# Merge stage on two pairs of PSUM banks, gated outputs transposed one gate later, output projection by halves of its inputs

## The chip, the cores and the metric

The kernel runs on one core of a Trainium2 chip. The metric is device time in microseconds (us). TensorE (PE) multiplies matrices and transposes; VectorE (DVE), ScalarE (ACT) and GpSimd (POOL) work elementwise; SyncE (SP) issues the transfers from HBM, in its program's order. Each engine works through its own instruction list in order and waits at semaphores for the others.

## The reference, cut to what matters

Two layers over 256 tokens of width 1024, all in float32. Each layer runs three causal mixers on one input projection, merges them by sigmoid gates, projects, normalises, and then runs a mixture of 32 experts.

```
proj = h @ w_in[l]           # all mixers' inputs, dn_gate, hg_gate, gate_logits
y_a = mla_branch(...)              @ w_br_a[l]
y_b = (rms_norm(dn_o) * silu(dn_gate)) @ w_br_b[l]   # gated DeltaNet
y_c = (rms_norm(hg_o) * silu(hg_gate)) @ w_br_c[l]   # HGRN2
g_a, g_b, g_c = split(sigmoid(gate_logits))
mixed = (g_a*y_a + g_b*y_b + g_c*y_c) @ w_out[l]
h = layer_norm(ALPHA*h + mixed)
# router: top-1 of 4 groups, then top-2 of its 8 experts; SwiGLU experts
h = layer_norm(ALPHA*h + hier_moe(h))
```

## The kernel before, in words

The 256 tokens are two tiles of 128 rows (t = 0, 1). A float32 product is made from three products of rounded halves (`mm3`, L261 to L263: high*high, low*high, high*low). A weight is split into its halves on the way: `split` lets ACT make the high half `wh` (L249) and DVE subtract to get the low half `wl` (L250); for the four names in `POOLED` POOL does the subtraction. `wh` and `wl` have two buffers each, so a split can run one piece ahead of PE. A tile of weights is 1 MB; in the merge stage it is split in two pieces, and each piece feeds 12 products (two token tiles, two blocks of 128 inputs, three products), which are called a chunk here.

The order per layer: the mixers (`seq` in `layer`); then branch a's gate and product in two column halves (`merge_branch`, c = 0, 1); the output gates of the two other branches, dn_gate and hg_gate (`gates`, `rows512`); `branch_gate` for dn and hg, which multiplies the normalised branch output by its gate (L1119), transposes it on PE in 16 blocks (L1126) and casts and splits the result (ACT L1128, DVE L1129); `router_sums` (a DVE reduction L568, a small product L571); `merge_branch` for b and c; the output projection `project_out` with the weights wo0 and wo1 (one for each half of the output columns); the router; the experts (`moe`, nine groups of experts, "quads"). glb0 names the gate of branch b, column half 0; br_b0 the product of branch b for that half. A merge step is: gate products, ACT tanh into `sg`, branch products, DVE (1 + sg) * product (L1277), POOL add to `mix` (L1279). `mix_turned` transposes `mix` into the projection's input, half by half of its columns.

PSUM results for t = 0 and t = 1 go to the banks named "pa" and "po", one bank each (`ps`, tag "pa"); the next step that uses them waits until ACT or DVE has read the last. Three banks are named "pm" and three "pb"; transposes and small products alternate between these names.

Weights come through SP's list in a fixed order into buffers: four in the pool `wp`, thirteen more that open when the mixers' memory closes (`open_prefetch`, `NPRE`), and five more that open at the end of the merge stage. A tile of one of the pools is loaded again when its last reader has finished; SP stands in line for that reader. The weight row tile `rows` (ln1_g and ln1_b for the first layer norm's scale, used by POOL's `scaled`, L376 and L377) uses such a buffer too. The order of instructions on each engine comes from a list scheduler with its own estimates; `issue_after` holds an instruction behind another.

Of the kernel before, what the change touches and what calls it, by code (L numbers as in the profile page):

```python
# [10 lines left out]
F32 = mybir.dt.float32  # L11
# [4 lines left out]
OP = mybir.AluOpType  # L16
# [91 lines left out]
class Trunk:  # L108
    def __init__(self, ctx, tc, A, out, dbg=None):
        self.ctx, self.tc, self.nc, self.A, self.out, self.dbg = ctx, tc, tc.nc, A, out, dbg or {}  # L110
        nc = self.nc
        pool = lambda n, b=1, **k: ctx.enter_context(tc.tile_pool(name=n, bufs=b, **k))
        self.cp = pool("consts")
        self.hp = pool("hidden")
        self.wp = pool("weights")
        self.wtiles, self.bufs = {}, {self.wp: self.NBUF}
        self.pk = pool("banks", space=PSUM)
        self.ctx_p, self.pp, self.nps, self.npa = ctx.enter_context(ExitStack()), None, 0, 0

    def cst(self, n, rows=slice(0, 128)):  # L120
        o, w = HOFF[n]
# [18 lines left out]
        return pool.tile([128, 512], F32, name="ps_" + tag, tag=tag, bufs=self.banks[tag])  # L140


    POOLED = {"cq.0", "cq.1", "gla00.0", "dn_gate1.1"}
    NBUF, NPRE = 4, 13
    BANKS, MIX_BANKS, MOE_BANKS = {"pa": 1, "pm": 3}, {"po": 1, "pb": 3}, {"sum": 4}
    NB = {"a2": 4, "a4": 7, "d2": 8, "d4": 7, "d8": 1, "wh": 2, "wl": 2, "o4": 4, "sg": 4}
# [140 lines left out]

    def wide(self, l, n, act):

        ps = [self.ps("pa") for _ in range(TB)]  # L290
        for i in range(2):
            self.wide_half(ps, l, n, act, i)
        return ps

    def wide_half(self, ps, l, n, act, i, ahead=False):
        self.dense_tm(ps, self.w(l, f"{n}{i}").rearrange("p (k c) -> p k c", k=4), act, f"{n}{i}", 4 * i, KT, ahead)
# [292 lines left out]
    def layer(self, l):  # L589
        tc, side = self.tc, dict(side="right")  # L590
        with ExitStack() as cl, ExitStack() as cr:
            self.ctx_l = cl
            self.sp = cr.enter_context(tc.tile_pool(name=f"split{l}", bufs=1, **side))
            self.gp = cr.enter_context(tc.tile_pool(name=f"merge{l}", bufs=1, **side))
            xp = cr.enter_context(ExitStack())
            hp = xp.enter_context(tc.tile_pool(name=f"x{l}", bufs=1, **side))
            oc = cr.enter_context(ExitStack())
            self.op = oc.enter_context(tc.tile_pool(name=f"o{l}", bufs=1, **side))
            with tc.tile_pool(name=f"mix{l}", bufs=1) as mp:
                self.mp = mp  # L600
                self.open_small(mp, 256)
                if l == 0:
                    rope, src = self.buf("d8", [128, 8, T]), self.A["positions"]
                    self.nc.sync.dma_start(rope[:, 0].bitcast(I32),
                                           bass.AP(tensor=src.tensor, offset=src.offset, ap=[[0, 128], [1, T]]))
                    self.issue(self.wp)
                self.mixer_consts(l, mp)
                if l == 0:
                    for _ in range(self.NBUF - 2):
                        self.issue(self.wp)  # L610
                    self.vrows = self.small_weights(l)
                self.mla_weights(l)
                gb = [x.rearrange("p h t -> p (h t)") for x in self.o4(F32)]
                for x, n in zip(gb, "gb"):
                    self.bcast_row(x, self.A["ln_in_" + n] if l == 0 else self.A["ln2_" + n][l - 1], D)
                self.hT = [hp.tile([128, KT, T], F32R, name=n, tag=n) for n in ("hTh", "hTl")]
                diag = self.gp.tile([128, 4, 128], F32, name="sg", tag="sg", bufs=self.NB["sg"])
                for t in range(TB):
                    self.nc.vector.tensor_scalar(diag[:, t], self.ident, self.hrs[:, t], None, op0=OP.mult)
                self.transposed(self.h, self.hT, self.gb0, tmp=lambda: self.buf("d2", [128, 2, T]), scale=diag)  # L620
                if l == 0:
                    with tc.issue_after(self.latest(self.nc.tensor)):
                        self.warm(8)
                    with tc.issue_after(self.last_lo.ins):
                        self.rope_tables(rope)
                self.router_weights(l)
                self.mix = self.gp.tile([128, TB, D], F32, name="mix")

                self.pq = self.ps("pm")
                self.chunk_cm(self.pq, l, "cq")  # L630
                seq = "dn_decay mla h0 dn_keys dn_inverse dn_queries h1 " \
                      "dn_values hg_forget hg_project hg_local dn_scan hg_scan"
                for n in seq.split():
                    f, a = (self.mla_heads, (int(n[1]),)) if n in ("h0", "h1") else (getattr(self, n), ())
                    self.bank = "pb" if n[:2] == "dn" else "pm"
                    f(l, mp, *a)
                    if f == self.mla:
                        with tc.issue_after(self.last_exp.ins):
                            for t in range(TB):
                                self.nc.scalar.activation(self.h[:, t], self.h[:, t], AF.Copy, scale=self.hrs[:, t])  # L640
                self.bank = None

                with tc.issue_after(self.latest(self.nc.gpsimd)):
                    self.scaled(self.h, gb[:1], gb[1:], self.nc.gpsimd)
                    if l == 0:
                        self.nc.gpsimd.tensor_copy(self.bits[:, 1], self.cst("ustrict"))
                self.dump(f"h2_{l - 1}", self.h.rearrange("p t d -> p (t d)"))
                self.merge_branch(l, "a")
                self.gates(l, mp)
                self.branch_gate(l, mp, "dn", self.dn_o)  # L650
                self.branch_gate(l, mp, "hg", self.hg_o)
                self.router_sums(self.last_gate.ins)
            self.pw = self.open_prefetch(f"prefetch{l}", self.NPRE)
            self.merge_branch(l, "b")
            def between():

                self.mixS = [hp.tile([128, 8, T], F32R, name=n, tag=n) for n in ("hTh", "hTl")]
                self.mix_turned(0)

            self.merge_branch(l, "c", between)  # L660

            oc.close()
            self.open_prefetch(f"more{l}a", 2)

            def free():
                xp.close()
                self.open_prefetch(f"more{l}b", 2)

            self.project_out(l, free)
            cr.close()  # L670
            self.open_prefetch(f"more{l}c", 1)
            with tc.tile_pool(name=f"h1_{l}", bufs=1, **side) as xp, tc.tile_pool(name=f"moe{l}", bufs=1, **side) as ep, \
                    ExitStack() as yc:
                self.moe(l, xp, ep, yc, self.h)
# [430 lines left out]
    def branch_gate(self, l, mp, n, o):  # L1105
# [10 lines left out]
            nc.vector.tensor_scalar(ss, ss, 1.0 / 128, 4 * EPS, op0=OP.mult, op1=OP.add)  # L1116
        self.rsqrt(rs, ss, self.small([128, 8]))
        for i in range(8):
            self.last_gate = nc.vector.scalar_tensor_tensor(ov[:, i], ov[:, i], rs[:, i:i + 1], gv[:, i], op0=OP.mult,  # L1119
                                                            op1=OP.mult)  # L1120
        oT = self.o4()
        for i in range(0, 4, 2):
            ps = self.ps()
# [133 lines left out]
            self.dump_oT(l, "mla")  # L1257


    def merge_branch(self, l, br, between=None):  # L1260


        nc = self.nc
        oT = self.oT[{"a": "mla", "b": "dn", "c": "hg"}[br]]
        for c in range(2):
            sg = [self.gp.tile([128, 512], F32, name="sg", tag="sg", bufs=self.NB["sg"]) for _ in range(TB)]
            for s, ps in zip(sg, self.wide(l, f"gl{br}{c}", self.hT)):
                nc.scalar.activation(s, ps, AF.Tanh, scale=0.5)
            if c and between:
                between()  # L1270
            n = f"br_{br}{c}"
            ps = [self.ps("pa") for _ in range(TB)]
            self.dense_tm(ps, self.w(l, n).rearrange("p (k c) -> p k c", k=4), oT, n, 0, 4)
            self.done(l, n)
            for t in range(TB):
# [15 lines left out]
    def project_out(self, l, free):  # L1291
        nc, A = self.nc, self.A

        r, st = self.h, self.stats(2)

        pr = self.ps()

        def route(t, c):
# [6 lines left out]
                nc.tensor.matmul(pr[:, 64 * t:64 * t + 36], x[:, k], self.rw[:, 4 * c + k, 0:36],  # L1305
                                 start=(t + c + k == 0), stop=(c + k == 4), skip_group_check=True)

        for c in range(2):
            ps = [self.ps("pa") for _ in range(TB)]
            for i in range(2):  # L1310
                self.wide_half(ps, l, f"wo{c}", self.mixS, i, c + i == 2)
                if c == 0 and i == 0:
                    self.mix_turned(1)
                if c == 1 and i == 0:
                    for t in range(TB):
                        route(t, 0)
            if c:
                free()
            cs = slice(512 * c, 512 * c + 512)
            for t in range(TB):  # L1320
                nc.vector.scalar_tensor_tensor(r[:, t, cs], self.h[:, t, cs], 2 * ALPHA, ps[t], op0=OP.mult, op1=OP.add)
                nc.vector.bn_stats(st[:, t, c], r[:, t, cs])
        for t in range(TB):
            route(t, 1)
        self.logits, self.st1 = pr, st


    def router(self, l, ep, x, xc):
# [446 lines left out]
```

## Time and profile before

| | before |
|---|---|
| median of 3 runs | 1159.97 us (1159.62 to 1160.34) |
| profiled execution, its own time | 1160.61 us |
| its span | 1158.8 us |
| PE busy | 1059.3 us, 91% |
| DVE, ACT, POOL busy | 50%, 37%, 14% |
| HBM over the span | 262 GB/s |

The two layers are alike: the second runs some 570 us after the first through the same steps. In layer 0 the gates' products end at 255.2 us, merge b and c run to 329 us, the output projection to 357.4 us, the router to 371 us and the experts to about 570 us. The start of a product minus the start of the one before it is the time that a product takes; what is above the usual value is a stall, also where the wait that the profile shows is shorter.

### The profile page before, as it was taken

How to read it: one execution, taken by the hardware profiler on the slowest of the kernel's cores; microseconds unless marked ns; L12 is line 12 of the kernel's file. 1: busy time of each engine (PE TensorE's matmuls, PEld its weight loads, DVE VectorE, ACT ScalarE, POOL GpSimd, SP SyncE). 2: the span in 40 equal slices, each digit the busy share in tenths (PEclk: the TensorE clock that was granted, in tenths of full speed). 3: DMA queues.
4: the chain of work that ended last, by engine and by line, in shares of the span. 5: the costliest groups of instructions: out<-in, count | busy, mean ns of one | idle time of the engine just before them, and what ended most of it. 6: DMA issues, size and time to landing. Idle time of an engine off the chain costs nothing. (4 is left out here: it accounts for less than half of the span.)

```text
span 1158.8 us, 21407 instructions
## 1 busy us (share of the span) xinstructions
PE 1059.3 (91%) x8896; PEld 775.6 (67%) x8896; DVE 576.9 (50%) x1269; ACT 427.3 (37%) x788; POOL 162.7 (14%) x146
## 2 busy tenths in 40 slices
PE   7999999999999998777889999999999999977775
PEld 5888987777777664434378889777777766543442
DVE  7677754575556422111276876645754562321114
ACT  5764632554445211111067545235444351211111
POOL 2111025101210400000020110450021112000001
PEclk9999999999999999898899999999999999989997
DMA  7632250549965999999983214315599679999994
GB/s 231 200 107 73 91 165 2 169 158 359 424 271 220 410 425 426 426 426 427 366 230 106 74 46 138 110 38 182 196 411 374 251 270 425 426 425 426 427 426 190
DMA packets 104706, 305.58 MB, mean 264 GB/s; under 512 B 20962, under 2 KB 48028, under 8 KB 79516
## 3 DMA queue, kind: packets, MB, share of 16 engines
q1 hardware_dynamic: 104604, 304.15, 68.4%
q8 instruction: 72, 1.18, 0.4%
q14 instruction: 30, 0.25, 0.1%
HBM read 303.08 MB, written 1.05 MB: 262 GB/s over the span
## 5 line engine op out<-in xcount | busy, mean ns | idle before, releaser
L250 DVE TENSOR_TENSOR wl<-w,wh 128x1024 fp32r<-128x1024 f32 x150 | 187.0, 1248 | 161.5 <-ACT wh L249 161.0
L249 ACT CAST wh<-w 128x1024 fp32r<-128x1024 f32 x158 | 165.7, 1049 | 217.7 <-PE ps_po L263 74.7
L1602 PE MATMUL ps_pa<-w,xg 128*32 128x256 f32 x2304 | 175.1, 436 | 59.0 <-DMA w<-in_exp_w_up_dram 29.4
L1602 PEld LDWEIGHTS ps_pa<-w,xg 128*32 128x32 f32 x2304 | 88.0, 125 | 140.4 <-DMA w<-in_exp_w_up_dram 38.2
L1614 DVE SCALAR_TENSOR_TENSOR hm<-ps_pa,ws,hm 128x256 f32<-128x256 f32 x18 | 8.7, 484 | 203.5 <-ACT hm L1613 203.3
L1613 ACT ACTIVATE hm<-ps_pa 128x256 f32<-128x256 f32 x18 | 6.9, 384 | 221.8 <-PE ps_pa L1602 221.8
L261 PE MATMUL ps_pa<-wh,hTh 128*128 128x512 f32 x176 | 71.2, 405 | 2.0 <-ACT hTh L254 0.7
L261 PE MATMUL ps_po<-wh,hTh 128*128 128x512 f32 x176 | 71.2, 405 | 1.9 <-ACT hTh L254 0.7
L262 PE MATMUL ps_po<-wl,hTh 128*128 128x512 f32 x176 | 70.5, 401 | 2.1 <-DVE wl L250 1.6
L262 PE MATMUL ps_pa<-wl,hTh 128*128 128x512 f32 x176 | 70.5, 401 | 2.1 <-DVE wl L250 1.6
L1635 PE MATMUL ps_pm<-w,hmT 128*32 128x512 f32 x576 | 70.8, 595 | 1.3 <-issue 1.3
L263 PE MATMUL ps_pa<-wh,hTl 128*128 128x512 f32 x176 | 70.0, 398 | 0.2 <-DVE hTl L255 0.2
L263 PE MATMUL ps_po<-wh,hTl 128*128 128x512 f32 x176 | 69.9, 397 | 0.2 <-DVE hTl L255 0.2
L1552 PEld LDWEIGHTS ps_pm<-P,h1c 128*128 128x128 f32 x576 | 66.8, 192 | 2.2 <-ACT res L1350 1.0
L1552 PE MATMUL ps_pm<-P,h1c 128*128 128x128 f32 x576 | 67.3, 275 | 0.0
L1561 ACT ACTIVATE xg<-ps_pm,gb 128x128 f32<-128x128 f32 x72 | 32.9, 458 | 71.7 <-DVE xg L1559 71.7
L1574 POOL TENSOR_TENSOR Pw<-P,small 128x128 f32<-128x128 f32 x32 | 12.4, 405 | 306.9 <-PE ps_pm L1581 227.9
L1279 POOL TENSOR_TENSOR mix<-mix,sg 128x512 f32<-128x512 f32 x16 | 28.3, 1792 | 155.4 <-DVE sg L1277 155.4
L1559 DVE TENSOR_SCALAR xg<-ps_pm,gb 128x128 f32<-128x128 f32 x72 | 29.4, 408 | 41.2 <-PE ps_pm L1552 32.2
L263 PE MATMUL ps_po<-hTh,wl 128*128 128x256 f32 (+1 forms) x168 | 48.7, 290 | 0.9 <-DVE wl L250 0.5
L263 PE MATMUL ps_pa<-hTh,wl 128*128 128x256 f32 (+1 forms) x168 | 48.9, 291 | 0.5 <-DVE wl L250 0.5
L261 PE MATMUL ps_pa<-hTh,wh 128*128 128x256 f32 (+1 forms) x168 | 49.2, 293 | 0.0
(442 smaller groups left out, 2134.9 us busy)
## 6 DMA issues: line engine op xcount, KB each, us to landing
w<-in_exp_w_gate_dram SPq DMA_DIRECT2D x66, 1024.0 KB
w<-in_exp_w_up_dram SPq DMA_DIRECT2D x66, 1024.0 KB
w<-in_exp_w_down_dram SPq DMA_DIRECT2D x64, 1024.0 KB
w<-in_w_in_dram SPq DMA_DIRECT2D x58, 1024.0 KB
w<-in_w_out_dram SPq DMA_DIRECT2D x8, 1024.0 KB
w<-in_w_br_a_dram SPq DMA_DIRECT2D x4, 1024.0 KB
w<-in_w_br_b_dram SPq DMA_DIRECT2D x4, 1024.0 KB
w<-in_w_br_c_dram SPq DMA_DIRECT2D x4, 1024.0 KB
```

What stands on the lines that cost most here:

```text
L249: nc.scalar.copy(v(hi), raw)
L250: engine.tensor_tensor(v(lo), raw, v(hi).bitcast(F32), op=OP.subtract)
L261: mm(ps, a[0], b[0], start=start, stop=False, skip_group_check=True)
L262: mm(ps, a[0], b[1], start=False, stop=False, skip_group_check=True)
L263: mm(ps, a[1], b[0], start=False, stop=stop, skip_group_check=True)
L1279: nc.gpsimd.tensor_tensor(mv, mv, sg[t], op=OP.add)
L1552: nc.tensor.matmul(ps[:, 128 * k:128 * k + 128], xc[:, t, 4 * h + k], Ps[q][:, t], start=(t == 0), stop=(t == 1))
L1559: nc.vector.tensor_scalar(xg[:, k], o, g, b, op0=OP.mult, op1=OP.add)
L1561: nc.scalar.activation(xg[:, k], o, AF.Identity, scale=g, bias=b)
L1574: self.pool_last = nc.gpsimd.tensor_tensor(e(Pw[:, t]), e(P[:, t]), w, op=OP.mult)
L1602: nc.tensor.matmul(pg[32 * e:32 * e + 32, FF * n:FF * n + FF], xgs[q][k // 4][:, k % 4, 32 * e:32 * e + 32], w[:, FF * k:FF * k + FF], sta ...
L1635: nc.tensor.matmul(ps[c][32 * e:32 * e + 32], hmT[:, i, 32 * e:32 * e + 32], ws[e][:, D * i + 512 * c:D * i + 512 * c + 512], start=(i == ...
```

## The change

What it does: `pair` gives a step either the banks pa and po or two of the pb banks, in turn, once merge a is done; so a gate and the branch product behind it lie on different banks. `branch_gate` ends at the multiplication; the transposes and casts (`branch_turned`) come behind the products of gate glb0, on pm banks. `project_out` takes half 0 of the inputs for both wo0 and wo1, then half 1 for each. The router's sums stand behind `hg_project`, in the scans. The subtraction for gla00's first and dn_gate1's second piece goes from POOL to DVE. The thirteen prefetch buffers open after the first gate of branch b.

```
-    POOLED = {"cq.0", "cq.1", "gla00.0", "dn_gate1.1"}
+    POOLED = {"cq.0", "cq.1"}
...
     def wide(self, l, n, act):
-        ps = [self.ps("pa") for _ in range(TB)]
+        ps = self.pair()
...
+    def pair(self):
+        self.npair += 1
+        return [self.ps("pb" if self.scans_done and self.npair % 2 else "pa") for _ in range(TB)]
...
                     f(l, mp, *a)
+                    if n == "hg_project":
+                        self.router_sums(self.latest(self.nc.vector))
...
                 self.merge_branch(l, "a")
+                self.scans_done = True
                 self.gates(l, mp)
                 self.branch_gate(l, mp, "dn", self.dn_o)
                 self.branch_gate(l, mp, "hg", self.hg_o)
-                self.router_sums(self.last_gate.ins)
+                first = self.merge_gate(l, "b", 0)
+                self.bank = "pm"
+                self.branch_turned(l, "dn", self.dn_o)
+                self.branch_turned(l, "hg", self.hg_o)
+                self.bank = None
             self.pw = self.open_prefetch(f"prefetch{l}", self.NPRE)
-            self.merge_branch(l, "b")
+            self.merge_branch(l, "b", gate=first)
...
-        for c in range(2):
-            ps = [self.ps("pa") for _ in range(TB)]
-            for i in range(2):
-                self.wide_half(ps, l, f"wo{c}", self.mixS, i, c + i == 2)
-                if c == 0 and i == 0:
-                    self.mix_turned(1)
-                if c == 1 and i == 0:
-                    for t in range(TB):
-                        route(t, 0)
-            if c:
-                free()
+        def residual(c):
             cs = slice(512 * c, 512 * c + 512)
             for t in range(TB):
...
+        ps = [self.pair() for _ in range(2)]
+        for c in range(2):
+            self.wide_half(ps[c], l, f"wo{c}", self.mixS, 0)
+            if c == 0:
+                self.mix_turned(1)
+        self.wide_half(ps[0], l, "wo0", self.mixS, 1)
+        residual(0)
+        for t in range(TB):
+            route(t, 0)
+        self.wide_half(ps[1], l, "wo1", self.mixS, 1, True)
+        free()
+        residual(1)
```

DVE, layer 0, between the splits of glb0's first and second chunk, before. The last row is the subtraction for the second chunk; `a_2193` is the hg branch's output, `o_2667` the low half of the dn branch's transposed output.

```order
L317 SCALAR_TENSOR_TENSOR a_2555<-a_2555,ps_po 128x512 [waits Activation_49]
L1129 SCALAR_TENSOR_TENSOR o_2667<-ps_pb,vcols,o_2666 128x512 [waits Activation_49]
L1129 SCALAR_TENSOR_TENSOR o_2667<-ps_pm,vcols,o_2666 128x512 [waits Activation_49]
L1119 SCALAR_TENSOR_TENSOR a_2193<-a_2193,small,a_2555 128x128 x2
L1119 SCALAR_TENSOR_TENSOR a_2193<-a_2193,small,a_2555 128x128 [waits DVE_49]
L1119 SCALAR_TENSOR_TENSOR a_2193<-a_2193,small,a_2555 128x128 x3
L568 TENSOR_REDUCE rsum<-rw 128x72
L250 TENSOR_TENSOR wl<-w,wh 128x1024 [waits Activation_49]
```

The same place after the change; the first `wl` is the second chunk's, the next the third's:

```order
L322 SCALAR_TENSOR_TENSOR a_2563<-a_2563,ps_pb 128x512 [waits Activation_49]
L1133 SCALAR_TENSOR_TENSOR a_2201<-a_2201,small,a_2563 128x128 x2
L1133 SCALAR_TENSOR_TENSOR a_2201<-a_2201,small,a_2563 128x128 [waits DVE_49]
L1133 SCALAR_TENSOR_TENSOR a_2201<-a_2201,small,a_2563 128x128 x3
L250 TENSOR_TENSOR wl<-w,wh 128x1024 [waits Activation_49]
L250 TENSOR_TENSOR wl<-w,wh 128x1024 [waits DMAHW5_49,Activation_49]
L1145 SCALAR_TENSOR_TENSOR o_2785<-ps_pm,vcols,o_2784 128x512 [waits Activation_49,Pool_49]
L1145 SCALAR_TENSOR_TENSOR o_2785<-ps_pm,vcols,o_2784 128x512 [waits Activation_49]
```

The two low halves (now L1145) have moved behind the splits of the second and the third chunk, and the reduction L568 is no longer here.

PE, layer 0, at the second chunk of glb0, before (`wh_2792` and `wl_2793` are that chunk's halves):

```order
L261 MATMUL ps_pa_2774<-wh_2792,hTh_194 128x512 [waits Activation_49]
L1126 MATMUL ps_pm_2727<-const_73,a4_2193 128x128 [waits DVE_49]
L1126 MATMUL ps_pm_2727<-const_73,a4_2193 128x128
L1126 MATMUL ps_pm_2727<-const_73,a4_2193 128x128 [waits DVE_49]
L261 MATMUL ps_po_2775<-wh_2792,hTh_194 128x512
L262 MATMUL ps_pa_2774<-wl_2793,hTh_194 128x512 [waits DVE_49]
L263 MATMUL ps_pa_2774<-wh_2792,hTl_195 128x512
```

After (`wh_2730` and `wl_2731` are the same chunk's halves):

```order
L261 MATMUL ps_pa_2712<-wh_2730,hTh_194 128x512 [waits Activation_49]
L261 MATMUL ps_po_2713<-wh_2730,hTh_194 128x512
L1142 MATMUL ps_pm_2786<-const_73,d4_2118 128x128 x4
L1142 MATMUL ps_pm_2793<-const_73,d4_2118 128x128 x4
L1142 MATMUL ps_pm_2802<-const_73,a4_2201 128x128 [waits DVE_49] x2
L262 MATMUL ps_pa_2712<-wl_2731,hTh_194 128x512 [waits DVE_49]
```

Ten of the sixteen transposes now stand between the products that need only `wh` and the first that needs `wl`; the other six come behind the gate.

SP, layer 0, in the experts' weights, shortly after the stream of loads restarts, before (`w_3721` is the `rows` tile, loaded six rows earlier):

```order
L195 DMA w_3764<-in_exp_w_up_dram 128x2048 [waits DMAHW2_49,PE_49]
L195 DMA w_3839<-in_exp_w_up_dram 128x2048 [waits DMAHW3_49,PE_49]
L195 DMA w_3841<-in_exp_w_up_dram 128x2048 [waits DMAHW4_49,PE_49]
L195 DMA w_3843<-in_exp_w_up_dram 128x2048 [waits DMAHW5_49,PE_49]
L195 DMA w_3845<-in_exp_w_down_dram 128x2048 [waits DMAHW6_49,PE_49]
```

After:

```order
L195 DMA w_3764<-in_exp_w_up_dram 128x2048 [waits DMAHW2_49,PE_49]
L195 DMA w_3839<-in_exp_w_up_dram 128x2048 [waits DMAHW4_49,DMAHW5_49,DMAHW3_49,Pool_49]
L195 DMA w_3841<-in_exp_w_up_dram 128x2048 [waits PE_49]
L195 DMA w_3843<-in_exp_w_up_dram 128x2048 [waits PE_49]
L195 DMA w_3845<-in_exp_w_down_dram 128x2048 [waits DMAHW6_49,PE_49]
```

The load of w_3839 now takes the buffer of the `rows` tile and waits for POOL, its last reader; before, a load twenty-one rows further down (w_4075) did. The second layer's list has the same exchange.

## Rows read from the trace of the kernel before

**Rows 1.** Page, part 1: busy time and share of the span by engine.

```profile
PE 1059.3 (91%) x8896; PEld 775.6 (67%) x8896; DVE 576.9 (50%) x1269; ACT 427.3 (37%) x788; POOL 162.7 (14%) x146
```

**Rows 2.** Waits of PE, 235 to 358 us: who waits, for whom, us, times, longest.

```profile
PE ps_pa L262 <- DVE wl L250: 1.6, 1, 1.6
PE ps_pa L261 <- ACT hTh L254: 0.7, 1, 0.7
PE ps_pa L262 <- POOL wl L250: 0.6, 1, 0.6
PE ps_pa L261 <- DVE sg L1277: 0.4, 2, 0.2
PE ps_pa L261 <- DVE res L1321: 0.3, 1, 0.3
```

**Rows 3.** Waits of PE, 805 to 928 us (layer 1).

```profile
PE ps_po L262 <- DVE wl L250: 1.6, 1, 1.6
...
```

**Rows 4.** Timeline of PE, pieces: start, us, engine, line, operands; idle before.

```profile
240.03 0.40 PE L261 MATMUL ps_pa<-wh,hTh 128*128 128x512 f32 x1
240.98 0.50 PE L262 MATMUL ps_pa<-wl,hTh 128*128 128x512 f32 x1 [0.56 <-POOL wl L250]
...
255.17 0.60 PE L1126 MATMUL ps_pb<-const,d 128*128 128x128 f32 x4
...
259.88 0.48 PE L261 MATMUL ps_po<-wh,hTh 128*128 128x512 f32 x1
261.92 0.50 PE L262 MATMUL ps_pa<-wl,hTh 128*128 128x512 f32 x1 [1.56 <-DVE wl L250]
...
275.47 0.40 PE L262 MATMUL ps_po<-wl,o 128*128 128x512 f32 x1
275.70 0.39 PE L263 MATMUL ps_po<-wh,o 128*128 128x512 f32 x1
276.27 0.47 PE L261 MATMUL ps_pa<-wh,hTh 128*128 128x512 f32 x1 [0.18 <-DVE sg L1277]
...
342.67 0.40 PE L263 MATMUL ps_po<-wh,hTl 128*128 128x512 f32 x1
343.35 0.47 PE L261 MATMUL ps_pa<-wh,hTh 128*128 128x512 f32 x1 [0.28 <-DVE res L1321]
```

**Rows 5.** Timeline of DVE, 253 to 263 us, pieces.

```profile
257.28 0.74 DVE L1129 SCALAR_TENSOR_TENSOR o<-ps_pm,vcols,o 128x512 fp32r<-128x512 f32 x1
...
259.51 1.22 DVE L568 TENSOR_REDUCE rsum<-rw 128x72 f32<-128x576 f32 x1
260.65 1.22 DVE L250 TENSOR_TENSOR wl<-w,wh 128x1024 fp32r<-128x1024 f32 x1
```

**Rows 6.** Timelines of POOL and DVE around 201 to 204 us.

```profile
201.18 2.38 POOL L377 TENSOR_TENSOR res<-res,o 128x1024 f32<-128x1024 f32 x1
203.50 3.40 POOL L377 TENSOR_TENSOR res<-res,o 128x1024 f32<-128x1024 f32 x1
202.43 2.20 DVE L250 TENSOR_TENSOR wl<-w,wh 128x1024 fp32r<-128x1024 f32 x1 [4.26 <-ACT wh L249]
```

**Rows 7.** Busy time by stretch; PEclk, DMA share and GB/s end each row.

```profile
322.00:376.00 54.00, 52.74 (x343) 40.51 (x345) 33.41 (x109) 26.60 (x38) 4.38 (x4) 1.00 0.61 235
376.00:394.00 18.00, 17.35 (x242) 11.54 (x238) 6.86 (x14) 3.39 (x7) 11.79 (x12) 1.00 1.00 392
...
456.00:570.00 114.00, 85.20 (x758) 44.36 (x759) 18.32 (x42) 10.53 (x22) 1.80 (x5) 0.87 1.01 425
```

**Rows 8.** Timelines of SP's queue and of POOL, 355 to 470 us, pieces.

```profile
375.05 0.33 SPq L195 DMA_DIRECT2D w<-in_exp_w_down_dram  x1
...
379.88 1.07 SPq L195 DMA_DIRECT2D w<-in_exp_w_up_dram  x1
387.04 1.28 SPq L195 DMA_DIRECT2D w<-in_exp_w_up_dram  x3
387.65 5.01 POOL L377 TENSOR_TENSOR res<-res,w 128x512 f32<-128x512 f32 x4
```

More of the change, by code (lines that the diff above doesn't have):

```diff
@@ L117, in __init__ @@
         self.pk = pool("banks", space=PSUM)
-        self.ctx_p, self.pp, self.nps, self.npa = ctx.enter_context(ExitStack()), None, 0, 0
+        self.ctx_p, self.pp, self.nps, self.npa, self.npair = ctx.enter_context(ExitStack()), None, 0, 0, 0
     def cst(self, n, rows=slice(0, 128)):
@@ L591, in layer @@
         with ExitStack() as cl, ExitStack() as cr:
-            self.ctx_l = cl
+            self.ctx_l, self.scans_done = cl, False
             self.sp = cr.enter_context(tc.tile_pool(name=f"split{l}", bufs=1, **side))
@@ L1118, in branch_gate, with branch_turned @@
         for i in range(8):
-            self.last_gate = nc.vector.scalar_tensor_tensor(ov[:, i], ov[:, i], rs[:, i:i + 1], gv[:, i], op0=OP.mult,
-                                                            op1=OP.mult)
+            nc.vector.scalar_tensor_tensor(ov[:, i], ov[:, i], rs[:, i:i + 1], gv[:, i], op0=OP.mult, op1=OP.mult)
+    def branch_turned(self, l, n, o):
+        nc = self.nc
         oT = self.o4()
@@ L1257, in mla_heads, with merge_gate, merge_branch @@
             self.dump_oT(l, "mla")
-    def merge_branch(self, l, br, between=None):
+    def merge_gate(self, l, br, c):
+        sg = [self.gp.tile([128, 512], F32, name="sg", tag="sg", bufs=self.NB["sg"]) for _ in range(TB)]
+        for s, ps in zip(sg, self.wide(l, f"gl{br}{c}", self.hT)):
+            self.nc.scalar.activation(s, ps, AF.Tanh, scale=0.5)
+        return sg
+    def merge_branch(self, l, br, between=None, gate=None):
         nc = self.nc
@@ L1265, in merge_branch @@
         for c in range(2):
-            sg = [self.gp.tile([128, 512], F32, name="sg", tag="sg", bufs=self.NB["sg"]) for _ in range(TB)]
-            for s, ps in zip(sg, self.wide(l, f"gl{br}{c}", self.hT)):
-                nc.scalar.activation(s, ps, AF.Tanh, scale=0.5)
+            sg = gate if gate and c == 0 else self.merge_gate(l, br, c)
             if c and between:
@@ L1271, in merge_branch @@
             n = f"br_{br}{c}"
-            ps = [self.ps("pa") for _ in range(TB)]
+            ps = self.pair()
             self.dense_tm(ps, self.w(l, n).rearrange("p (k c) -> p k c", k=4), oT, n, 0, 4)
@@ L1294, in project_out @@
         r, st = self.h, self.stats(2)
+        self.bank = "pm"
         pr = self.ps()
@@ L1306, in route @@
                                  start=(t + c + k == 0), stop=(c + k == 4), skip_group_check=True)
-        for c in range(2):
-            ps = [self.ps("pa") for _ in range(TB)]
-            for i in range(2):
-                self.wide_half(ps, l, f"wo{c}", self.mixS, i, c + i == 2)
-                if c == 0 and i == 0:
-                    self.mix_turned(1)
-                if c == 1 and i == 0:
-                    for t in range(TB):
-                        route(t, 0)
-            if c:
-                free()
+        def residual(c):
             cs = slice(512 * c, 512 * c + 512)
             for t in range(TB):
-                nc.vector.scalar_tensor_tensor(r[:, t, cs], self.h[:, t, cs], 2 * ALPHA, ps[t], op0=OP.mult, op1=OP.add)
+                nc.vector.scalar_tensor_tensor(r[:, t, cs], self.h[:, t, cs], 2 * ALPHA, ps[c][t], op0=OP.mult, op1=OP.add)
                 nc.vector.bn_stats(st[:, t, c], r[:, t, cs])
+        ps = [self.pair() for _ in range(2)]
[10 more added lines that the diff above has]
+        residual(1)
         for t in range(TB):
             route(t, 1)
-        self.logits, self.st1 = pr, st
+        self.logits, self.st1, self.bank = pr, st, None
     def router(self, l, ep, x, xc):
```

## The prediction

> **What bounds the kernel now.** I read the page's first part, then PE's waits in the stretch that the change rewrites, then PE's timeline there, then the table by stretch. PE is busy for 91% of the span [rows 1], so the question is where it pauses, and whether a pause taken away there moves the end. Between the last gate product and the end of the output projection the waits of PE are few and short: 1.6 us for a low half of a weight, 0.7 for the projection's transposed input, 0.6 for a low half made by POOL, 0.4 for the sums that read the banks, 0.3 for the residual [rows 2]. Layer 1 shows the same list at the same sizes [rows 3]. The list understates: products start every 0.23 us (275.47, 275.70), so a start 0.57 later is a stall of 0.34, where only 0.18 is called a wait, and the product behind a pause is about 0.1 late as well [rows 4]. I count by starts.
>
> After this stretch comes the experts' stage. Late in it the DMA queues are full (share 1.01) while PE is busy 85.2 of 114 us [rows 7], so transfers set its end. They stand still before it, though: from 322 to 376 us the share is 0.61, 0.39 * 54 = 21 us of idle transfer time, because the buffers are full. The stream restarts at 375.05, when PE's first expert products free a buffer [rows 7, 8], and is full from then on. So an earlier PE means an earlier restart, and time saved in the merge stage should reach the layer's end.
>
> **The change part by part, layer 0.** All by starts in rows 4.
>
> The split of dn_gate's last piece on POOL: 0.95 between two starts instead of 0.23, 0.72, and 0.1 behind it: 0.8 goes. A DVE subtraction takes 1.22 [rows 5]; POOL stops being the wait. Bounds 0 and 0.8; I take 0.8.
>
> glb0's second chunk: 2.04 between starts, a stall of 1.8. The subtraction starts at 260.65, behind the reduction (1.22) and two low halves of 0.74 [rows 5]; in the new order these stand elsewhere, so it could start some 2.6 earlier, at about 258.1, and end at 259.3. PE arrives earlier too: six of sixteen transposes no longer stand before it, at 0.60 / 4 = 0.15 at most each, 0.7 with overlap. It would stand ready at 259.9 + 0.2 - 0.7 = 259.4. So both arrive together, and I count the whole 1.8. If the subtraction is 0.5 later than I think, 1.3 is left; that is the lower bound, and 1.9 the upper.
>
> The banks: four places per layer where a gate or the projection waits for the sums that read the last branch product. One is shown, 0.57 - 0.23 = 0.34; with the late product behind it 0.4. Four are 1.5, the last being smaller. With two pairs of banks each has been read a whole step (11 or 6 us) before. Layer 1 has a fifth, behind merge a, 0.4, since there the parity puts dn_gate on the other pair.
>
> The projection: its transposed input is waited for 0.7 [rows 2], and its low half and the late products make it 1.3 by starts; now 24 products of wo1 lie between the transposes and their first use, 24 * 0.23 = 5.6 us, and they cover ACT and DVE's work. Between wo0 and wo1, 0.68 - 0.23 and the late product, 0.5; it goes, since wo1 has banks of its own. The router's transposes of the first half come two chunks before the end as they did, with the sums of the residual directly before them; I add 0.1.
>
> Sum of what goes: 0.8 + 1.8 + 1.5 + 1.3 + 0.5 = 5.9 in layer 0, 6.3 in layer 1.
>
> What is added. ACT has two casts of the hg branch in front of the split for br_b0's second chunk: 0.3, between 0 and 1.5 (both whole, if they take the 0.74 that DVE needs for the same tiles [rows 5]). In the scans DVE gets the reduction and one subtraction, 1.22 each [rows 5], and two small operations; a subtraction that stood between two of the scan's steps moves behind them, so most of it should fit. I take 0.4, between 0 and 2.8 (all of it on the scan's chain). The prefetch opens later, since the transposes now follow glb0's last product: by 24 products at most, 5.6 us. The 21 us of idle transfers [rows 7] hide this; without them it would cost the 5.6.
>
> DVE and POOL also meet there. At 202.43 a subtraction took 2.20 instead of 1.22, while POOL's next operation took 3.40 and the one before it 2.38 [rows 5, 6]: DVE stood until POOL's operation ended at 203.5, then POOL's next stood for DVE's. The Trainium skill, "SBUF — State Buffer", section "Who interferes with whom", says that a DVE instruction with two inputs in SBUF contends with a GpSimd instruction that reads SBUF, and that the loser of the shared ports is blocked for the whole instruction, not slowed. By that rule the trace agrees, and it speaks against taking the subtraction off POOL where POOL multiplies for the scan: were each layer to lose 2.38 once, the time would be 4.8 us higher than I forecast. The new subtraction should fall into a pause of POOL's, so I add nothing for it; the bound of 2.8 stands for both.
>
> Net: 5.9 - 0.8 = 5.1 and 6.3 - 0.8 = 5.5, 10.6 in all. The profiled execution took 1160.61 us with a span of 1158.8; 1160.6 - 10.6 = 1150.0. That execution is 0.64 above the median of the runs, so against the median 1149.4.
>
> **The rivals.** First, half the gain. Where PE no longer pauses for a bank, it may pause for the weights: the cast on ACT, the subtraction of 1.22 [rows 5] and the hand-overs must fit into a chunk's 12 * 0.23 = 2.8 us, and DVE's sums (two per step) sit in the same list. For: glb0's stall was of this kind. Against: no other chunk shows one now. It would take back the 1.5 of the banks and about 1.2 elsewhere, 2.7 per layer: 1149.4 + 5.4 = 1154.8.
>
> Second, no change: the stall goes, but the experts' end is set by transfers. For: share 1.01 while PE idles [rows 7]. Against: the restart hangs on PE [rows 8]. Then 1160.
>
> Third, slower, by one load. In the new order the load of w_3839 takes the buffer that POOL's scaling reads, and SP stands there with the whole stream behind it. Before, it was issued at 387.04; POOL's last operation ends at 387.65 + 5.01 = 392.66 [rows 8], 5.6 later. From 375.05 to 380.95 seven loads' worth of about 1.05 MB have been issued (the first and the last are in rows 8; one half-sized pair among them): 7.3 MB. From 376 to 394 the queues moved 18 * 392 = 7.1 MB [rows 7], so what is issued lasts until about 394.6, and the next load, issued at 392.7, starts about 1.1 later (an estimate from the first issue at 375.05 and queues that are full from 376 on), at 393.8. So the wait is hidden by 0.8 us, and I cost it at nothing; but the cover is thin. If the queued loads covered nothing, each layer would lose 5.6 + 1.1 = 6.7, 13.4 in all, against 10.6 gained: 1162.8. It decides against the change from 5.3 us of idle queue per layer on.
>
> **How the numbers follow.** The forecast, 1149.4, has 0.72, with its own range of 1146.5 to 1152.5 (the bounds of glb0, the casts and the scans). Half the gain has 0.15, no change 0.06, slower 0.07. The range is 1146 to 1156.5: it takes in the first rival and leaves the others out. About 0.2%, 2.3 us, is what can be told from no change: faster means under 1157.6. Faster: 0.72 + 0.15 = 0.87; the same 0.07; slower 0.06.
>
> **What would show it.** Right: PE's waits for sums at the gates and for the projection's input are gone, glb0's second chunk starts its low-half product within 0.3 of its place, the projection ends 5 us earlier in layer 0 and 10.5 in layer 1 (counting the first layer's gain), and the stream restarts as much earlier. Wrong: new waits for `wl` in merge b and c of over 0.3 each; DMA share under 0.95 around 18 us after the restart, with SP waiting for POOL's scaling; the scans ending more than 1 us later than before; or an experts' stage that grows by what the merge gave.

## The result, and the profile after

The changed kernel takes 1148.38 us (median of 4 runs, 1146.39 to 1150.61) against 1159.8 for the one before (4 runs): ratio 0.9904, interval 0.989 to 0.9917. The forecast was 1149.4. Run again beside a later version it took 1149.16 (ratio 0.9907, 0.9893 to 0.9921).

The first part of the page after, to be set beside [rows 1]:

```profile
PE 1055.0 (92%) x8896; PEld 773.2 (67%) x8896; DVE 584.3 (51%) x1273; ACT 427.7 (37%) x788; POOL 149.2 (13%) x142
```

PE does the same number of products in a span that is 12.3 us shorter (1146.5 us). The waits of PE after the change, from 235 to 360 us (who waits, for whom, us in total, times, longest), have one row where [rows 2] has five:

```profile
PE ps_pa L262 <- DVE wl L250: 0.5, 1, 0.5
```

The waits for POOL's low half, for the sums at the banks, for the projection's input and for the residual are all gone. The one row that is left is new, and not the one of [rows 2]; it is read below. Layer 1 shows the same single row.

PE's timeline after, at the two places that gave most, glb0's second chunk [rows 4] and the projection's input (start, us, operation, operands):

```profile
256.06 0.40 PE L261 MATMUL ps_pa<-wh,hTh 128*128 128x512 f32 x1
256.29 0.39 PE L261 MATMUL ps_po<-wh,hTh 128*128 128x512 f32 x1
256.52 1.04 PE L1142 MATMUL ps_pm<-const,d 128*128 128x128 f32 x8
257.40 0.38 PE L1142 MATMUL ps_pm<-const,a 128*128 128x128 f32 x2
257.55 0.50 PE L262 MATMUL ps_pa<-wl,hTh 128*128 128x512 f32 x1
...
330.41 0.39 PE L263 MATMUL ps_po<-wh,hTl 128*128 128x512 f32 x1
330.64 1.03 PE L1308 MATMUL ps_pm<-const,mix 128*128 128x128 f32 x8
331.43 0.48 PE L261 MATMUL ps_pb<-wh,hTh 128*128 128x512 f32 x1
```

At 257.55 the second chunk of glb0 goes on with its low half straight behind ten transposes; before, 2.04 us lay there between two starts. At 331.43 the products of wo1 follow the transposes of `mix` at once, where before PE stood for their cast:

```profile
336.74 0.50 PE L261 MATMUL ps_pa<-wh,hTh 128*128 128x512 f32 x1 [0.75 <-ACT hTh L254]
```

The experts' stream restarts as much earlier. SP's queue and POOL after, to be set beside [rows 8]:

```profile
368.84 0.33 SPq L195 DMA_DIRECT2D w<-in_exp_w_down_dram  x1
...
386.52 1.52 SPq L195 DMA_DIRECT2D w<-in_exp_w_up_dram  x3
```

```profile
381.48 5.01 POOL L382 TENSOR_TENSOR res<-res,w 128x512 f32<-128x512 f32 x4
```

The restart comes at 368.84, 6.21 earlier. The wait that the third rival was built on is there: the load behind POOL's scaling goes out at 386.52, when POOL's last operation ends (381.48 + 5.01 = 386.49); SP's waits from 366 to 400 us put 9.6 us down to POOL in one piece (the view names Pw, the operation that starts as the scaling ends):

```profile
SPq L195 <- POOL Pw L1599: 9.6, 1, 9.6
```

What it cost is read from the table by stretch (busy times of the engines, then PEclk, DMA share, GB/s):

```profile
376.00:386.00 10.00, 9.35 (x130) 4.75 (x132) 4.76 (x10) 2.55 (x5) 9.82 (x8) 1.00 1.02 429
386.00:388.00 2.00, 2.00 (x44) 1.23 (x40) 0.00 (x0) 0.00 (x0) 1.22 (x3) 1.00 0.97 401
388.00:390.00 2.00, 2.00 (x21) 1.42 (x14) 0.48 (x1) 0.38 (x1) 0.00 (x0) 1.00 0.92 385
390.00:392.00 2.00, 2.00 (x20) 2.00 (x20) 0.41 (x1) 0.02 (x1) 0.00 (x0) 1.00 1.01 406
```

The queues dip to 0.97 and 0.92 for two steps of 2 us and are full again: 0.03 and 0.08 of 2 us each, or 0.2 us of transfer time. The loads in flight covered the wait, barely.

**Where the time went.** ACT casts the weights piece by piece (L249, 158 casts), in the same order in both programs, so the n-th cast is a milestone. Start in the kernel before minus start after, in us:

| milestone (start after) | gained so far | this step | forecast |
|---|---|---|---|
| mixers, 150.5 | 0.53 | 0.53, not of the change | |
| merge a, 230.5 | 0.82 | scans 0.29 | -0.4 |
| output gates, 247.8 | 1.92 | dn_gate's subtraction 0.82, a bank between dn_gate and hg_gate 0.28 | 0.8, none |
| br_b0's second chunk, 272.5 | 3.66 | glb0 and the moved transposes 1.74 (0.37 of the late casts' cost taken off) | 1.8 |
| glb1, 278.8 | 3.35 | one bank 0.42, a new wait -0.73 | bank 0.4, casts -0.3 |
| wo0, 328.0 | 4.32 | three banks 0.97 | 1.1 |
| wo1's first half, 334.5 | 5.78 | transposed input 1.46 | 1.3 |
| last half, 340.1 | 6.30 | wo0 to wo1 0.52 | 0.5 |
| layer 1, 571.5 | 6.63 | experts 0.33 | 0 |
| layer 1's mixers, 657.8 | 6.31 | -0.32 | 0 |
| layer 1's last cast, 906.7 | 12.58 | merge of layer 1, 6.27 | 5.5 |

The first row arises in the first 50 us, and the profiles of the other versions stand from 0.3 earlier to 0.9 later than this one at this milestone; it says nothing on the change.

### The profile page after: what moved, and what is told of

Its sections match the earlier page's. It is cut to its first block, busy times and chain, and to the rows that moved or that the text cites. A ratio compares the mean times of both kernels' runs of the same rounds, so it can differ in the third digit from the quotient of the medians.

```text
span 1146.5 us, 21394 instructions
## 1 busy us (share of the span) xinstructions
PE 1055.0 (92%) x8896; PEld 773.2 (67%) x8896; DVE 584.3 (51%) x1273; ACT 427.7 (37%) x788; POOL 149.2 (13%) x142
## 5 line engine op out<-in xcount | busy, mean ns | idle before, releaser
L250 DVE TENSOR_TENSOR wl<-w,wh 128x1024 fp32r<-128x1024 f32 x154 | 193.8, 1261 | 144.1 <-ACT wh L249 143.1
L249 ACT CAST wh<-w 128x1024 fp32r<-128x1024 f32 x158 | 165.7, 1049 | 205.0 <-PE ps_po L263 52.3
L1627 PEld LDWEIGHTS ps_pa<-w,xg 128*32 128x32 f32 x2304 | 84.6, 124 | 142.0 <-DMA w<-in_exp_w_up_dram 38.2
L1599 POOL TENSOR_TENSOR Pw<-P,small 128x128 f32<-128x128 f32 x32 | 12.3, 404 | 302.6 <-PE ps_pm L1606 227.9
L262 PE MATMUL ps_pb<-wl,hTh 128*128 128x512 f32 x128 | 51.0, 398 | 0.5 <-DVE wl L250 0.5
L263 PE MATMUL ps_pb<-wh,hTl 128*128 128x512 f32 x128 | 50.8, 397 | 0.0
L261 PE MATMUL ps_pb<-wh,hTh 128*128 128x512 f32 x128 | 50.4, 398 | 0.0
L255 DVE TENSOR_TENSOR Yl<-ps_pm,Yh 128x512 fp32r<-128x512 f32 x36 | 24.8, 689 | 48.6 <-ACT Yh L254 48.6
L1660 PEld LDWEIGHTS ps_pm<-w,hmT 128*32 128x32 f32 x576 | 21.0, 109 | 42.3 <-issue 32.4
L261 PE MATMUL ps_po<-hTh,wh 128*128 128x256 f32 (+1 forms) x168 | 48.6, 290 | 0.1
```

Source lines behind the costliest of these rows:

```text
L249: nc.scalar.copy(v(hi), raw)
L250: engine.tensor_tensor(v(lo), raw, v(hi).bitcast(F32), op=OP.subtract)
L255: self.last_lo = (engine or self.nc.vector).tensor_tensor(lo, src, hi.bitcast(F32), op=OP.subtract)
L261: mm(ps, a[0], b[0], start=start, stop=False, skip_group_check=True)
L262: mm(ps, a[0], b[1], start=False, stop=False, skip_group_check=True)
L263: mm(ps, a[1], b[0], start=False, stop=stop, skip_group_check=True)
```

## The experiments

All are edits of the changed kernel, whose median to compare with is 1148.4. The kernel before, run again beside each group of them, had medians of 1159.4, 1158.9 and 1160.6, so a difference of medians is known to about 1 us. Milestones are read from one profile of each.

**The four subtractions back on POOL.**

```
-    POOLED = {"cq.0", "cq.1"}
+    POOLED = {"cq.0", "cq.1", "gla00.0", "dn_gate1.1"}
```

> The changed kernel, with the four subtractions given back to POOL. Theory (each stall counted in its own place reaches the end): dn_gate's last piece again makes PE wait, 1.1 us per layer by the changed kernel's trace, and in the scans nothing more than 0.3 changes, so 2 to 2.8 us more than the changed kernel: about 1150.8. In its trace a wait of 0.5 to 0.6 for POOL's low half near 241 us. Rival (the experts' transfers set the end whatever the merge does): no more than 0.5 us more, with the wait there all the same.

Measured: 1155.65 us (9 runs; ratio to before 0.9963, 0.9951 to 0.9975), 7.3 more than the changed kernel, far above both. By milestones dn_gate gave back 0.82 per layer, less than the expected 1.1, since that step also held the bank wait of 0.28. The rest was lost in the scans: 1.7 in layer 0 and 3.3 in layer 1. DVE, POOL and PE there, in layer 0:

```profile
164.18 3.56 DVE L1061 TENSOR_TENSOR a<-a 128x256 f32<-128x256 f32 x2
```

```profile
162.17 3.73 POOL L250 TENSOR_TENSOR wl<-w,wh 128x1024 fp32r<-128x1024 f32 x1 [46.33 <-ACT wh L249]
166.10 1.50 POOL L1058 TENSOR_TENSOR a<-a,a 128x512 f32<-128x512 f32 x1 [0.20 <-PE ps_pm L1039]
```

```profile
168.53 0.40 PE L261 MATMUL ps_po<-wh,hTh 128*128 128x512 f32 x1
170.99 0.28 PE L1039 MATMUL ps_pm<-a,a 128*64 128x64 f32 x2 [2.06 <-DVE a L1061]
```

The two multiplications on DVE in the changed kernel, and POOL's subtraction in the kernel before:

```profile
165.11 0.41 DVE L1061 TENSOR_TENSOR a<-a 128x256 f32<-128x256 f32 x1
167.41 0.28 DVE L1061 TENSOR_TENSOR a<-a 128x128 f32<-128x128 f32 x1
```

```profile
162.30 2.40 POOL L250 TENSOR_TENSOR wl<-w,wh 128x1024 fp32r<-128x1024 f32 x1 [46.67 <-ACT wh L249]
```

Two multiplications of the scan, 0.41 and 0.28 us in the changed kernel, took 3.56 here, beside POOL's subtraction and the multiplication behind it, which ends at 167.60. The subtraction took 3.73 instead of 2.40, and PE waited 2.06. It is the blocking of [rows 6] again, with more at stake. In layer 1 PE's clock fell after the same pause (busy times by stretch; PEclk is the third number from the end):

```profile
738.00:740.00 2.00, 1.35 (x36) 1.38 (x37) 1.45 (x5) 0.00 (x0) 0.06 (x1) 1.00 0.79 234
740.00:742.00 2.00, 2.00 (x10) 1.67 (x9) 1.97 (x3) 0.00 (x0) 2.00 (x2) 0.50 0.75 290
742.00:744.00 2.00, 2.00 (x7) 1.44 (x6) 0.51 (x1) 0.09 (x1) 0.68 (x1) 0.65 0.00 0
```

**The router's sums late again.**

```
-                    if n == "hg_project":
-                        self.router_sums(self.latest(self.nc.vector))
...
                 self.branch_gate(l, mp, "hg", self.hg_o)
+                self.bank = "pm"
+                self.router_sums(self.latest(self.nc.vector))
```

> The changed kernel, with the router's sums behind the output gates again (transposes stay late). Theory (glb0's stall came from DVE's list, and the reduction of 1.2 stood directly ahead of the subtraction): a stall of about 1.2 at glb0's second chunk comes back in each layer, and the scans change by less than 0.4: 2 to 2.8 us more than the changed kernel, about 1150.6. Rival (the late transposes alone took the stall away): under 0.6 us more.

Measured: 1153.34 us (9 runs; ratio 0.9956, 0.9941 to 0.9971), 5.0 more. The place is the theory's: DVE and PE at glb0, with the reduction directly ahead of the subtraction:

```profile
256.27 1.21 DVE L573 TENSOR_REDUCE rsum<-rw 128x72 f32<-128x576 f32 x1
257.40 1.22 DVE L250 TENSOR_TENSOR wl<-w,wh 128x1024 fp32r<-128x1024 f32 x1
```

```profile
256.29 0.39 PE L261 MATMUL ps_po<-wh,hTh 128*128 128x512 f32 x1
258.67 0.50 PE L262 MATMUL ps_pa<-wl,hTh 128*128 128x512 f32 x1 [1.99 <-DVE wl L250]
```

The pause is 2.15 by starts, longer than the reduction; the scheduler now also put the transposes elsewhere, and PE had nothing between. By milestones layer 0 lost 2.4 at glb0 and won back 0.7 at glb1, whose wait does not arise in this run, so 1.6 in the merge stage; layer 1 lost 3.2 there, since the clock fell after the pause. The scans lost 0.3 in each layer. The clock in layer 1:

```profile
828.00:830.00 2.00, 2.00 (x7) 1.54 (x6) 0.00 (x0) 0.20 (x1) 0.00 (x0) 0.50 0.98 368
```

So the late transposes alone did not take the stall at glb0 away, and the rival falls. The stall that came back was twice the theory's 1.2; how much of it is the reduction's alone, and how much the missing transposes between, these runs do not part.

**Both together, so that the scans run as before the change.**

```
+    POOLED = {"cq.0", "cq.1", "gla00.0", "dn_gate1.1"}
...
+                self.router_sums(self.latest(self.nc.vector))   # late, as above
```

> The changed kernel, with the four subtractions on POOL and the router's sums late, so that the scans run as before the change. In the run with the subtractions on POOL and the sums early, the scans lost 1.7 us in layer 0 and 3.3 in layer 1: two multiplications of the scan on DVE took 3.56 us beside POOL's subtraction. Theory (the reduction pushes these multiplications into POOL's subtraction, and the shared port holds them; in layer 1 the pause also drops PE's clock): without the reduction both losses go, 5.0 less, and 1.2 per layer comes back at glb0: 1155.7 - 5.0 + 2.4 = 1153.1. Rival (POOL's subtraction costs the scans this much by itself): 1155.7 + 2.4 = 1158.1.

Measured: 1156.28 us (11 runs; ratio 0.9972, 0.9961 to 0.9982), between the two. The milestones part it: the scans lose 0.3 in each layer (as with the sums late alone), instead of 1.7 and 3.3, as the theory has it; most of what is above its 1153.1 lies in the merge stage behind the pause at glb0, 3.1 in layer 0 (pause and fallen clock) and 1.6 in layer 1. POOL's subtraction alone does not hurt the scans; it does together with the early reduction, which moves DVE's multiplications into it.

**The gated outputs transposed early again.**

```
+                self.bank = "pm"
                 self.branch_gate(l, mp, "dn", self.dn_o)
+                self.branch_turned(l, "dn", self.dn_o)
                 self.branch_gate(l, mp, "hg", self.hg_o)
+                self.branch_turned(l, "hg", self.hg_o)
+                self.bank = None
                 first = self.merge_gate(l, "b", 0)
-                self.branch_turned(...)   # both
```

> The changed kernel, with the transposes and casts of both branches ahead of glb0 again, on pm banks; the router's sums stay in the scans. Theory (the stall at glb0 was DVE's list: the reduction 1.2 and two low halves 1.3 ahead of the subtraction): the low halves are back, the reduction is not, so 0.5 to 1.3 us of stall per layer come back, while the new wait at br_b0's gate (0.6) goes: between 0 and 1.5 us more in all, about 1149.2. Rival (the transposes alone made the stall): the whole 1.8 per layer comes back, 3.6 us more, about 1152.

Measured: 1148.14 us (4 runs; ratio 0.9905, 0.9889 to 0.992), no difference. A wait of 0.46 us stands at glb0 instead of the one at glb1; by milestones 0.4 is lost at glb0 and 0.7 won at glb1, so the merge is 0.3 shorter in each layer. (Layer 0's experts took 2.9 longer in this profile, the largest difference of this kind here.) This part of the change brings nothing by itself.

**One pair of banks in the merge.**

```
-        return [self.ps("pb" if self.scans_done and self.npair % 2 else "pa") ...]
+        return [self.ps("pb" if self.turns and self.npair % 2 else "pa") ...]   # turns: set in project_out
```

> The changed kernel, with the gates, branch products and output gates on pa and po alone; the output projection keeps two pairs. Theory: the waits for the sums come back, 4 in layer 0 and 5 in layer 1 at 0.3 to 0.45 each, 1.4 and 1.8 us: 3.2 us more, about 1151.6. Rival (without the bank the weights' split is what PE waits for): the pauses only change their name, under 1 us more.

Measured: 1153.71 us (5 runs; ratio 0.9952, 0.9938 to 0.9965), 5.3 more. By milestones the merge gave back 1.48 in layer 0 and 1.75 in layer 1, the theory's 1.4 and 1.8; the other 2 us lie in the first 50 us and in layer 0's experts, where profiles differ by as much. The size by the clock is therefore not settled to better than 2 us; the place is.

**The output projection in the old order, on two pairs.**

```
-        ps = [self.pair() for _ in range(2)]
+        for c in range(2):
+            ps = self.pair()
+            for i in range(2):
+                self.wide_half(ps, l, f"wo{c}", self.mixS, i, c + i == 2)
```

> The changed kernel, with the output projection in the old order (wo0 whole, then wo1), its two results still on different pairs of banks. Theory: the wait for the transposed input comes back, 1.46 us per layer, the wait between wo0 and wo1 (0.5) does not: 2.9 us more, about 1151.3. Rival (the order and the banks of wo1 are one gain): 4 us more, about 1152.4.

Measured: 1152.19 us (5 runs; ratio 0.9943, 0.9929 to 0.9956), 3.8 more; by milestones 1.6 and 1.7 in the two projections, 3.3. The wait of 0.8 for the transposed input is back, none between wo0 and wo1. The median, 1152.19, lies nearer the rival's 1152.4 than the theory's 1151.3 and decides nothing; the place of the waits decides for the theory. PE's waits from 235 to 360 us:

```profile
PE ps_pa L261 <- ACT hTh L254: 0.8, 1, 0.8
PE ps_pa L262 <- DVE wl L250: 0.5, 1, 0.5
PE ps_pa L263 <- DVE hTl L255: 0.2, 1, 0.2
```

**A longer PE ahead of the experts.**

```
-        self.warm(26)
+        self.warm(48)
```

> The changed kernel, with 22 more filling products of PE (no result uses them) in the router's pause, ahead of the selection, 0.22 us each. Theory (the transfers restart with PE's first expert products, so what delays PE ahead of them reaches the end): 22 * 0.22 = 4.8 us per layer more, less what the router's chain leaves idle, so 8 to 9.7 us more, about 1157.5. Rival (the experts' transfers set the end and have slack): under 2 us more.

Measured: 1158.42 us (12 runs; ratio 0.9992, 0.9983 to 1.0001), 10 more. SP's queue:

```profile
374.36 0.33 SPq L195 DMA_DIRECT2D w<-in_exp_w_down_dram  x1
```

The stream restarts at 374.36 instead of 368.84, 4.7 of it from the products (0.8 is the profile's later start). The span is 10.6 longer, 9.8 beyond that start, where two layers of 4.7 make 9.4. So what PE loses ahead of the experts does reach the end, and the second rival falls.

**The hg casts later.** The wait that is left stands at glb1's first chunk. PE, DVE and POOL of the changed kernel there:

```profile
275.08 0.40 PE L261 MATMUL ps_pa<-wh,hTh 128*128 128x512 f32 x1
275.94 0.50 PE L262 MATMUL ps_pa<-wl,hTh 128*128 128x512 f32 x1 [0.46 <-DVE wl L250]
```

```profile
273.55 2.33 DVE L250 TENSOR_TENSOR wl<-w,wh 128x1024 fp32r<-128x1024 f32 x1 [0.40 <-ACT wh L249]
```

```profile
272.25 2.56 POOL L1300 TENSOR_TENSOR mix<-mix,sg 128x512 f32<-128x512 f32 x2 [64.94 <-DVE sg L1298]
```

The subtraction takes 2.33 instead of 1.23: the casts of the hg branch push it into POOL's addition.

```
+        def cast():   # the ACT and DVE casts of branch_turned, returned and called later
...
-            self.merge_branch(l, "b", gate=first)
+            self.merge_branch(l, "b", later, gate=first)   # hg's cast, behind gate glb1
```

> The changed kernel, with the casts of the hg branch's transposed output (ACT and DVE) issued behind the gate of branch b's second half. Theory: the only wait of PE left in the merge stage, 0.46 us called (0.7 by starts) at glb1's first chunk, comes from these casts, which push a subtraction into POOL's add to mix; with them gone it goes: 1.4 us less, about 1147.0. Rival (POOL's add takes the port whenever it runs): the wait moves to another subtraction, within 0.4 of the changed kernel.

Measured: 1146.92 us (5 runs; ratio 0.9893, 0.9877 to 0.9908). No wait of PE is left from 235 to 360 us, and by milestones each layer wins 1.1, more than the 0.7 said: the second chunk of br_b0 had been late as well, by 0.37. The median alone, 1.5 less, is no more than the spread of the medians.

**Two pairs of banks from merge a on, with the late hg casts.**

```
+            if br == "a" and c == 0:
+                self.scans_done, self.npair = True, 0
```

> The changed kernel, with the hg casts behind the gate of branch b's second half, and the two pairs of banks in use from merge a's first branch product on. Theory: beside the wait for the casts (1.07 us per layer in the run with the casts alone), the waits for the sums behind merge a go, at 213 and 231 us in layer 0 (0.33 and 0.41 with 0.17 behind them, 0.9) and one in layer 1 (0.4): 2.1 + 1.3 = 3.4 us less than the changed kernel, about 1145.0. Rival (pb banks are still wanted by the scans' last steps): the merge's first product waits for them, and what is won is at most the casts' 2.1.

 

> The changed kernel itself, run beside the next one. Theory and rival alike: its time of before, 1148.4, give or take 1; the first 50 us differ by up to 1 us from profile to profile, as the kernels so far did.

Measured side by side: 1145.53 us (4 runs; ratio 0.9871, 0.9856 to 0.9887) against 1149.16 for the changed kernel, 3.6 less. By milestones the casts give 1.1 per layer, merge a 0.9 in layer 0 and 0.4 in layer 1. The scans' last steps did not need the pb banks. This is the fastest of all, 15 us below the kernel before.

## Why the prediction was right, point by point

**The bound.** That PE's pauses in the merge stage reach the end through the restart of the stream was argued from idle queues [rows 7]; the longer filling products showed it: 4.7 us of PE per layer became 9.8 of span.

**dn_gate's subtraction.** Put at 0.8, gave 0.82, and cost 0.82 when it went back.

**glb0.** The sum was right, 1.74 for 1.8 (2.11 before the 0.37 of the casts in the same step), and the working half right. That the subtraction stood behind DVE's reduction and two low halves [rows 5] holds, and the late sums show that the late transposes alone do not remove the stall. The low halves, put at twice 0.74, count for little: with them early again and the reduction gone, a wait of 0.46 stands at glb0, the one of 0.46 at glb1 goes, and the time is the same.

**The banks.** 1.39 by milestones in layer 0 for 1.5, and 0.28 at a fifth place, between dn_gate and hg_gate, that the text did not name; undone, 1.48 and 1.75.

**The projection.** 1.46 and 0.52 for 1.3 and 0.5; undone by order alone, 1.6 and 1.7, with no wait between wo0 and wo1, as two causes should do.

**What is added.** The casts ahead of br_b0 were put at 0.3 and cost 1.1, within the bound of 1.5: the text saw ACT's list and not that the delayed subtraction would meet POOL's addition. The scans were put at -0.4 and came out at +0.3 per layer. That term had the wrong sign. The 0.3 arises ahead of POOL's subtraction at 162.30, in PE's order. Before, and after:

```profile
157.93 0.40 PE L261 MATMUL ps_po<-wh,hTh 128*128 128x512 f32 x1
158.26 0.34 PE L1025 MATMUL ps_pm<-a,a 128*64 128x64 f32 x4
158.53 0.50 PE L262 MATMUL ps_pa<-wl,hTh 128*128 128x512 f32 x1
```

```profile
157.46 0.39 PE L261 MATMUL ps_po<-wh,hTh 128*128 128x512 f32 x1
157.68 0.49 PE L262 MATMUL ps_pa<-wl,hTh 128*128 128x512 f32 x1
```

Four of the scan's small products no longer stand between these wide ones, 0.60 between two starts becomes 0.22, and nothing is lost behind. Both runs with the sums late lose the 0.3 again, with the subtraction on DVE or on POOL, and the run with the subtractions alone on POOL keeps it up to that subtraction. So it goes with the reduction's place in the scheduler's order, which the prediction did not weigh, and that it came out as a gain is luck. The text asked what two more operations cost on DVE's list there, and weighed the port only as a danger. In the trace of before, DVE stood still in the scan beside POOL's subtraction:

```profile
164.79 0.75 DVE L1027 COPY_PREDICATED a<-mconst,ps_pm 128x512 f32<-128x512 int32 x1 [2.39 <-POOL wl L250]
```

Those 2.39 us of DVE may have been the room for both operations; that is argued, not shown. The Trainium skill's rule in "SBUF — State Buffer", section "Who interferes with whom", that a two-input DVE operation and a reading GpSimd operation shut each other out, was read in the prediction as speaking against taking the subtraction off POOL. The trace agrees with the rule (3.56 us for two multiplications of 0.69 together), but it speaks the other way: with the early reduction, leaving it on POOL costs 1.7 and 3.3 us; with the late one it costs the scans nothing.

**The rivals.** Half the gain: the one new wait for a low half is of that rival's kind, 0.73 per layer and not 2.7. No change: fell with the filling products. Slower: its wait is real, 9.6 us of SP, and its price was rightly put at almost nothing, 0.2 us of transfer time. So two of the signs that the prediction named as wrong did appear, a new wait of over 0.3 for a low half and a DMA share under 0.95 with SP waiting for POOL, at a small price. How much longer POOL would have to take before it decides was not tried. The prefetch that opens later cost nothing that shows: no wait for a load is among PE's waits from 235 to 360 us.

The two layers gave 5.77 and 6.27 where 5.1 and 5.5 were forecast. In layer 0 the scans came out 0.7 better than forecast, glb0 0.3 and the banks 0.2, and the casts 0.8 worse. That the sum lies so near is in part luck: errors of both signs in it partly cancel.

## What to carry to other kernels

Count stalls by the starts of neighbouring instructions, undo each part alone, and compare by milestones in the trace: one stage outside the change, layer 0's experts, differed by up to 2.9 us between profiles here. When work moves between VectorE and GpSimd, look at what the other of the two runs at that moment, and not only at the length of the list it joins. Of several parts of a change one can bring nothing (here the late transposes) or depend on another (the early sums need the subtraction off POOL); single undoings show it.

## What the runs showed of the hardware that was not expected

A pause of PE of about 2 us was sometimes followed by a lower granted clock: after waits of 1.99 to 2.07 us, the rows show 0.50 (1.2 GHz) for some 3.3 us, with products 0.43 apart instead of 0.23, in layer 1 of two runs (the subtractions on POOL, the sums late) and in layer 0 of a third (both together), and 1.00 throughout in the other layer of the same three profiles. Each fall cost 1.5 to 1.6 us on top of the pause, by the milestones of the two layers. The waits of 1.6 us at glb0 before the change [rows 2, 3] were followed by no fall. So a pause of this length has two prices, and removing it also removes a part of the spread between runs; that last step is argued, not shown.
